# Norms by pairs of columns, first products interleaved, and low parts of weights by accumulating DMA, in a two-part transformer on one core

## The chip, the cores and the metric

The kernel runs on one core of a Trainium2 chip. The metric is the device time of one launch in microseconds, by the median of several runs; the profiled execution is one more run. TensorE does the matrix products (PE), VectorE (DVE), ScalarE (ACT) and GpSimd (POOL) the rest; SyncE (SP) issues most of the DMAs.

## The reference

A first block of two layers (differential attention with the modulation of both contexts, then neighbourhood attention, each followed by an MLP) hands x, 512 tokens of width 1024, to a second block of two layers. All of it is float32.

```python
def second_block(x, meta_tokens, w_in, w_ret_o, ...):
    h = jnp.concatenate([meta_tokens, x], axis=1)             # 16 + 512 tokens
    for l in range(DEPTH):
        u = rms_norm_2(h, norm_mix_pre[l])
        proj = u @ w_in[l]                                    # split into q, k, v, g of both branches, two gates
        ...
        y_r = retention_branch(...) @ w_ret_o[l]
        y_a = attention_branch(...) @ w_att_o[l]
        mix = (jax.nn.sigmoid(gate_r) * y_r + jax.nn.sigmoid(gate_a) * y_a) @ w_mix_o[l]
        h = h + rms_norm_2(mix, norm_mix_post[l])
        u = rms_norm_2(h, norm_ff_pre[l])
        ff = jnp.square(jax.nn.relu(u @ w_ff1[l])) @ w_ff2[l]
        h = h + rms_norm_2(ff, norm_ff_post[l])
    return h[:, N_META:]
```

## The kernel before

Activations lie transposed, 128 features by tokens, eight tiles k deep. Float32 products are made of three: every operand is a high part rounded to PE's format and a low part, the rest (`split` L214 for activations, by ACT and DVE), and `mm3` (L219, its matmul is L228) adds high x high, high x low and low x high. bigB and bigC are the high and low part of a normed input; bigA, the residual; bigD and bigF another such pair.

Weights come through `wring` (L235): SP loads a [128, 1024] tile `wr` (512 KB), ACT copies it into the high part `wh` (L207), and another engine, POOL unless the call names one, subtracts it to give the low part `wl` (L253):

```python
            self.act(h[:, c], r[:, c], AF.Copy)
            ...
                eng.tensor_tensor(l[:, q], r[:, q], h[:, q].bitcast(F32), op=ALU.subtract)
```

There are five buffers of `wh` and `wl` and two of `wr` (eight and three in the MLP stages).

The tokens are worked in two groups (`eg`: 272 or 256 tokens, and 256). A stage ends in a norm: `rstd` (L375) squares the eight k on ACT into `nt`, adds them on DVE into `na`, sums over partitions with a product by `ones` on PE (L384) into `n`, and makes 1/sqrt on ACT into `nr`. `norm_gain` (L399, L403) and `norm_mod` (L390) multiply and split into bigB and bigC, k by k. In `block2` the part behind the mix products (L1375 on) does this for the post-norm (L1393, the old residual `xo` loaded just before it) and the norm of the MLP; `after` (L1412) does it at the end of a layer, where half of the additions to bigA run on POOL (L1421) and `b2_norm` and `front` (L1086) begin the next layer with the first products of `k`, `q` and two gates.

`mlp` (L796) goes over eight chunks c of the hidden width, each with four first products (`first`), a squared relu into `hh` and `hl`, and eight second ones. In chunks 1 to 6 of three of the four MLPs `product7` (L853) takes seven products of sums of weights and inputs in place of eight. The sums of inputs (`sums`, L826) are made behind chunk 0, k by k, by POOL and DVE in turn; those of weights by POOL (L269).

The order on each engine is set by a scheduler from the program's text and its own estimates of durations; each engine then takes its instructions in that order. A tile's buffers are handed out in turn, so an instruction that writes a tile also waits for the readers of the tile that had the buffer before.

Stages, in us of the profiled execution: the first block to about 1520, its last output products and norm to 1640, MLP to 1885, front to 1945, then for the first layer of the second block retention to 2175, attention to 2335, mix to 2400, mix products, norms and chunk 0 to 2565, MLP to 2835, end norms and front to 2945; for the second layer retention to 3110, attention to 3268, mix to 3360, norms and chunk 0 to 3500, MLP to 3760, end.

Of the kernel before, what the change touches and what calls it, by code (L numbers as in the profile page):

```python
# [10 lines left out]
F32 = mybir.dt.float32  # L11
F32R = mybir.dt.float32r
BF16 = mybir.dt.bfloat16
AF = mybir.ActivationFunctionType
# [160 lines left out]
class Program:  # L175
# [59 lines left out]
    def wring(self, *parts, size=1024, low=None, eng=None):  # L235
# [10 lines left out]
        def parts(r, c, eng):  # L246
# [9 lines left out]
        def load(src, c=slice(0, size)):  # L256

            r = raw()
            self.nc.sync.dma_start(r[:, c], src)
            return parts(r, c, eng or self.G)  # L260
# [113 lines left out]

    def rstd(self, pl, X, n):  # L375

        pv = self.pt("n")[:, :n]
        acc = self.tl(pl, "na", [128, self.nw], 1)[:, :n]
        for k in range(8):
            sq = acc if k == 0 else self.tl(pl, "nt", [128, self.nw], self.nb)[:, :n]  # L380
            self.act(sq, X[:, k], AF.Square)
            if k:
                self.tt(acc, acc, sq, ALU.add)
        self.T.matmul(pv, self.ones, acc, start=True, stop=True)  # L384
        r = self.tl(pl, "nr", [128, self.nw], self.nb // 2)[:, :n]
# [4 lines left out]
    def norm_mod(self, pl, i, c, X, n, j, hh, hl):  # L390
        A, B = self.modA[i, c + 1], self.modT[i][:, c]
        r = self.rstd(pl, X, n)
        for k in range(8):
# [5 lines left out]
    def norm_gain(self, pl, X, n, g, hh, hl):  # L399
        r = self.rstd(pl, X, n)  # L400
        for k in range(8):
# [21 lines left out]
    def decays(self, pl):  # L423
# [10 lines left out]
        for c in (slice(0, 528), slice(528, 1055)):  # L434
            n = c.stop - c.start
            d = self.tl(pl, "delta", [16, 528], 1)[:, :n]
            nc.scalar.dma_start(d, self.ap["delta"][:, c].to_broadcast([16, n]))
            f = self.tl(pl, "fdec", [16, 528], 1)[:, :n]
# [6 lines left out]
    def layer0(self):  # L445
# [5 lines left out]
        with st:  # L451
            wp = st.enter_context(self.phase("l0w"))
            load = self.wring((wp, 5, 2), size=768)
# [26 lines left out]
            with self.psum(n=(1, 2), pj=(1, 6)), self.phase("l0n") as pn:  # L480
                self.nw, self.nb = 512, 4
# [241 lines left out]
    def post(self, i):  # L723
# [13 lines left out]
        with self.psum(a=(1, 6), n=(1, 2)), self.phase("pw") as wp, self.phase("post") as pl:  # L737
            load = self.wring((wp, 8, 2), eng=V) if both else self.wring((self.wp, 5, 2), (wp, 3, 1))
            self.nw, self.nb = (512, 3) if both else (336, 5)
# [56 lines left out]
    def mlp(self, pl, load, w1, w2, width, gs, fin, after, fast=None, before=None):  # L796
# [21 lines left out]

        def second(m, c, us, gs, hid):
# [6 lines left out]
        def sums():  # L826
# [782 lines left out]
```

## Time and profile before

| what | us |
|---|---|
| median of 3 runs | 3780.08 (3775.22 to 3780.64) |
| the profiled execution | 3780.57 |
| its span | 3778.6 |
| PE busy | 3476.2 (92%) |
| DVE busy | 2447.4 (65%) |
| POOL busy | 1938.6 (51%) |
| ACT busy | 1892.2 (50%) |

Busy shares are means over the whole span, in which stages with different limits follow each other. PE's 92% leaves about 300 us in which it does nothing; beside that, a product lasts longer when the granted clock (PEclk, 1.00 is full speed) is low. A wait names the engine, the line and what it waited for.

### The profile page before, as it was taken

The numbers are of one execution on the slowest core, as the hardware profiler recorded it, in microseconds if no ns is written. First come the engines' busy times: TensorE is split into PE (matmuls) and PEld (weight loads), VectorE is DVE, ScalarE is ACT, GpSimd is POOL, SyncE is SP. The second block draws the span as 40 slices with busy tenths as digits, with TensorE's granted clock in tenths as the row PEclk, the third lists the DMA queues.
The fourth block names the chain that finished last, engine by engine and source line by source line (L and its number), as shares of the span: only waits on it lengthen the run. The fifth ranks groups of instructions, "written<-read, shape, count | busy, mean of one in ns | idle before, by whom it ended". The sixth has DMA issues, their size and how long they took to land.

```text
span 3778.6 us, 58735 instructions
## 1 busy us (share of the span) xinstructions
PE 3476.2 (92%) x22512; PEld 3186.2 (84%) x22512; DVE 2447.4 (65%) x4189; ACT 1892.2 (50%) x3915; POOL 1938.6 (51%) x1754
## 2 busy tenths in 40 slices
PE   7888888899999999799989999979997999998998
PEld 6788876778888998788889899979997888787888
DVE  5666657433335777777677666496667767558766
ACT  5777755332125877533346665443334666543333
POOL 5778765442002665587732332457763233356884
PEclk9999999999999999999999999989998999999999
DMA  5222133442112222223322221323332222241333
GB/s 196 74 73 73 59 104 99 140 134 95 56 56 73 58 61 67 81 90 95 123 95 71 78 76 52 116 78 95 96 124 84 82 89 73 59 135 64 101 95 106
DMA packets 118571, 338.04 MB, mean 89 GB/s; under 512 B 13905, under 2 KB 37330, under 8 KB 118034
## 3 DMA queue, kind: packets, MB, share of 16 engines
q1 hardware_dynamic: 105664, 315.97, 26.7%
q10 hardware_dynamic: 12626, 18.32, 1.5%
q8 instruction: 176, 2.88, 0.3%
q14 instruction: 105, 0.86, 0.1%
HBM read 321.39 MB, written 12.86 MB: 88 GB/s over the span
## 4 chain that ended last, share of the span: by engine, by line
PE 49%; DVE 18%; POOL 13%; DMA 7%; ACT 6%; issue 6%; ACTq 0%; POOLq 0%; SPq 0%; DVEq 0%
PE a L228 38%; POOL wmu L345 9%; DMA wmg<-in_wmod 5%; PE pj L228 4%; DVE ms L888 3%; POOL wl L253 2%; DVE hl L217 2%; DVE ms L212 1%; DVE nt L212 1%; ACT wh L207 1%; DVE na L212 1%; PE po L1311 1%; ACT wmu L209 1%; DVE bigC L217 1%; DVE nt L403 1%
## 5 line engine op out<-in xcount | busy, mean ns | idle before, releaser
L253 POOL TENSOR_TENSOR wl<-wr,wh 128x256 fp32r<-128x256 f32 (+3 forms) x568 | 994.3, 1770 | 1031.8 <-ACT wh L207 902.7
L207 ACT ACTIVATE wh<-wr 128x1024 fp32r<-128x1024 f32 (+3 forms) x560 | 536.0, 972 | 731.8 <-PE a L228 387.4
L228 PE MATMUL a<-bigB,wh 128*128 128x256 f32 (+3 forms) x2140 | 637.3, 316 | 27.0 <-ACT bigB L216 17.2
L228 PE MATMUL a<-bigC,wh 128*128 128x256 f32 (+3 forms) x2140 | 645.6, 316 | 7.6 <-DVE bigC L217 7.6
L228 PE MATMUL a<-bigB,wl 128*128 128x256 f32 (+3 forms) x2140 | 642.1, 315 | 0.4 <-DVE wl L253 0.4
L345 POOL TENSOR_TENSOR wmu<-wmg,sc 128x256 f32<-128x256 f32 x512 | 420.3, 852 | 268.6 <-DMA wmg<-in_wmod 196.2
L228 PE MATMUL a<-hl,wh 128*128 128x256 f32 (+2 forms) x1664 | 492.8, 333 | 23.3 <-DVE hl L217 23.2
L228 PE MATMUL a<-hh,wh 128*128 128x256 f32 (+2 forms) x1664 | 466.2, 333 | 42.7 <-ACT hh L216 33.1
L228 PE MATMUL a<-hh,wl 128*128 128x256 f32 (+2 forms) x1664 | 487.0, 331 | 0.0
L228 PEld LDWEIGHTS a<-bigB,wh 128*128 128x128 f32 x2140 | 397.6, 193 | 54.4 <-ACT bigB L216 19.1
L228 PEld LDWEIGHTS a<-bigC,wh 128*128 128x128 f32 x2140 | 399.5, 192 | 33.8 <-DVE bigC L217 10.2
L228 PEld LDWEIGHTS a<-bigB,wl 128*128 128x128 f32 x2140 | 399.0, 193 | 24.7 <-DVE wl L253 1.1
L228 PEld LDWEIGHTS a<-hh,wh 128*128 128x128 f32 x1664 | 287.4, 192 | 81.1 <-ACT hh L216 38.2
L228 PEld LDWEIGHTS a<-hl,wh 128*128 128x128 f32 x1664 | 296.6, 193 | 63.6 <-DVE hl L217 35.4
L253 DVE TENSOR_TENSOR wl<-wr,wh 128x1024 fp32r<-128x1024 f32 (+1 forms) x144 | 201.0, 1405 | 184.8 <-ACT wh L207 184.3
L228 PEld LDWEIGHTS a<-hh,wl 128*128 128x128 f32 x1664 | 296.3, 193 | 27.2
L228 PE MATMUL a<-bigF,wh 128*128 128x256 f32 (+3 forms) x1024 | 295.0, 294 | 2.3 <-ACT bigF L216 2.3
L217 DVE TENSOR_TENSOR hl<-ms,hh 128x512 fp32r<-128x512 f32 (+4 forms) x160 | 190.2, 1207 | 80.0 <-ACT hh L216 79.4
L209 ACT ACTIVATE wmu<-wmu 128x1024 f32<-128x1024 f32 x128 | 135.3, 1057 | 201.7 <-POOL wmu L345 201.0
L228 PEld LDWEIGHTS a<-bigF,wh 128*128 128x128 f32 x1024 | 194.2, 192 | 5.3 <-ACT bigF L216 2.5
L228 PE MATMUL a<-bigD,wh 128*128 128x256 f32 (+2 forms) x640 | 187.2, 303 | 6.6 <-ACT bigD L216 4.1
L228 PE MATMUL pj<-wh,bigB 128*128 128x384 f32 x512 | 182.2, 360 | 9.8 <-ACT raw L207 5.6
(350 smaller groups left out, 8541.3 us busy)
## 6 DMA issues: line engine op xcount, KB each, us to landing
wr<-in_w SPq DMA_DIRECT2D x128, 512.0 KB, 3.6
wr<-in_wf SPq DMA_DIRECT2D x128, 512.0 KB, 3.6
wmg<-in_wmod SPq DMA_DIRECT2D x80, 512.0 KB, 3.6
wr<-in_wfm SPq DMA_DIRECT2D x76, 512.0 KB, 3.5
wr<-in_wqkv SPq DMA_DIRECT2D x64, 384.0 KB, 3.2
wm<-in_wmod SPq DMA_DIRECT2D x16, 512.0 KB, 6.2
wr<-in_wv SPq DMA_DIRECT2D x16, 512.0 KB, 3.5
wr<-in_wret SPq DMA_DIRECT2D x16, 512.0 KB, 3.5
```

Of the source, the lines that this page charges most:

```text
L207: self.S.activation(o, i, f, bias=bias, scale=scale)
L209: self.S.activation(o, i, f, bias=bias, scale=scale, accum_out=accum)
L212: self.V.tensor_tensor(o, a, b, op=op)
L217: self.V.tensor_tensor(lo, src, hi.bitcast(F32), op=ALU.subtract)
L228: self.T.matmul(o, w, x, start=(i == 0 and j == 0), stop=(i == n - 1 and j == 2))
L253: eng.tensor_tensor(l[:, q], r[:, q], h[:, q].bitcast(F32), op=ALU.subtract)
L345: self.G.tensor_tensor(u[:, q:q + 256], w[:, q:q + 256], self.sc[:, j, q:q + 256], op=ALU.mult)
L403: self.V.scalar_tensor_tensor(t, X[:, k], g[:, k:k + 1], r, op0=ALU.mult, op1=ALU.mult)
L888: V.scalar_tensor_tensor(r[:, s], r[:, s], 0.0, r[:, s], op0=ALU.max, op1=ALU.mult)
L1311: T.matmul(po[g], x[:n, t - 1], y[:, s], start=False, stop=(t == 4 and j == 2))
```

## The change

All code of the second block, and the first block's second `post`, is touched; the first block's other stages keep their form (the calls there get `eng=G` and `pairs = False`).

Weights: with `eng=None` the low part is made by ACT (l = -h) and a DMA from POOL's queue that reads the weight again and adds it. This holds for all loads of front, retention, attention and mix (62 a layer) and for the eight weights of chunk 0 in three MLPs. Weights of the mix products (`wmix`) have their low part made on DVE.

```diff
+            if eng is None:
+                self.act(l[:, c], h[:, c].bitcast(F32), AF.Copy, scale=-1.0)
+                self.G.dma_start(l[:, c], src, accum_op=ALU.add)
+                return h, l
...
-        load = self.wring((self.wp, 5, 2))
+        load = self.wring((self.wp, 5, 2), eng=None)
...
+            how = dict(eng=None) if c == 0 and fast else {}
+            u1 = [(load.sums if quick else load)(w1[c * 4 + j], **how) for j in range(4)]
+            u2 = [load(w2[c * 4 + j], **how) for j in range(4)]
...
+            us = [load(ap["wmix"][li, m], eng=V) for m in range(8)]
```

Norms: two k at a time, [128, 544] tiles; the gain moves to the instruction behind.

```diff
+    def scaled(self, pl, X, r, n):
+
+        for k in range(0, 8, 2):
+            u = self.pair(pl, "nt", n)
+            self.tt(u, X[:, k:k + 2], r[:, None].to_broadcast([128, 2, n]), ALU.mult)
+            yield from ((k + i, u[:, i]) for i in range(2))
...
+            acc = self.pair(pl, "na", n, 1)
+            for k in range(0, 8, 2):
+                sq = self.pair(pl, "nt", n) if k else acc
+                self.act(sq, X[:, k:k + 2], AF.Square)
+                if k:
+                    self.tt(acc, acc, sq, ALU.add)
+            for i in range(2):
+                self.T.matmul(pv, self.ones, acc[:, i], start=(i == 0), stop=(i == 1))
...
-        for k in range(8):
-            t = self.tl(pl, "nt", [128, self.nw], self.nb)[:, :n]
-            self.V.scalar_tensor_tensor(t, X[:, k], g[:, k:k + 1], r, op0=ALU.mult, op1=ALU.mult)
-            self.split(hh[:, k], hl[:, k], t)
+        for k, u in self.scaled(pl, X, r, n):
+            self.act(hh[:, k], u, AF.Copy, scale=g[:, k:k + 1])
+            self.V.scalar_tensor_tensor(hl[:, k], u, g[:, k:k + 1], hh[:, k].bitcast(F32),
+                                        op0=ALU.mult, op1=ALU.subtract)
```

The post-norm takes the old residual from prefetched tiles (`old`: `hh`, `hl`, `rr`, `gr`; 12 DMAs a layer from POOL's queue); the end norm adds in the same instruction.

```diff
+            for m in range(8):
+                t = self.tl(pl, ("hh", "hl")[m % 2], [128, 528], 4)[:, :n0]
+                G.dma_start(t, spill[:, m, eg[0]])
...
+                t = self.tl(self.b5, ("rr", "gr")[m // 4], [128, 528], 2)[:, :2 * n1].rearrange("p (k t) -> p k t", k=2)
+                G.dma_start(t, spill[:, m:m + 2, eg[1]])
...
-                    xo = self.tl(pl, "xo", [128, 272], 3)[:, :n]
-                    nc.sync.dma_start(xo, spill[:, m, s])
...
+                for m, u in self.scaled(pl, A[:, :, s], r, n):
+                    V.scalar_tensor_tensor(A[:, m, s], u, g[:, m:m + 1], old[i][m], op0=ALU.mult, op1=ALU.add)
...
-                    V.scalar_tensor_tensor(t, Df[:, m, s], g[:, m:m + 1], r, op0=ALU.mult, op1=ALU.mult)
-                    (V, G)[m % 2].tensor_tensor(A[:, m, s], A[:, m, s], t, op=ALU.add)
+                for m, u in self.scaled(pl, Df[:, :, s], r, n):
+                    V.scalar_tensor_tensor(A[:, m, s], u, g[:, m:m + 1], A[:, m, s], op0=ALU.mult, op1=ALU.add)
```

`sums` works on pairs of k, all on DVE (28 instructions), and `norm_mod` on pairs too. Products between stages: `first2` (chunk 0) and `mmu2` (front) run two units k by k.

```diff
+        def first2(us, j, g, hid):
+
+            x = g[3]
+            ps = [self.pt("a")[:, :x.stop - x.start] for _ in range(2)]
+            for k in range(8):
+                for i, p in enumerate(ps):
+                    wh, wl = block(us, j + i, k)
+                    for y, (w, z) in enumerate(((wh, g[1]), (wh, g[2]), (wl, g[1]))):
+                        T.matmul(p, w, z[:, k], start=(k + y == 0), stop=(k == 7 and y == 2))
...
-        for _, u in units:
-            u.start()
-            u.run(u.groups[:1])
+        for a, b in ((units[0][1], units[1][1]), (units[2][1], units[3][1])):
+
+            for u in (a, b):
+                u.start()
+            for u, p in zip((a, b), mmu2(a.w, b.w, (a.groups[0], b.groups[0]))):
+                self.act(u.raw[:, u.groups[0]], p, AF.Copy)
```

DVE's order behind the mix products of the first layer, group 0, before (the numbers are of buffers, `na` the sum of squares, `nr` 1/sqrt):

```order
L212 TENSOR_TENSOR na_25437<-na_25437,nt_25451 128x272
L212 TENSOR_TENSOR na_25437<-na_25437,nt_25454 128x272
L212 TENSOR_TENSOR na_25437<-na_25437,nt_25457 128x272
L1393 SCALAR_TENSOR_TENSOR nt_25466<-bigA_72,vecs,nr_25461 128x272
L1393 SCALAR_TENSOR_TENSOR nt_25471<-bigA_72,vecs,nr_25461 128x272
L1393 SCALAR_TENSOR_TENSOR nt_25476<-bigA_72,vecs,nr_25461 128x272
L1393 SCALAR_TENSOR_TENSOR nt_25481<-bigA_72,vecs,nr_25461 128x272
L1393 SCALAR_TENSOR_TENSOR nt_25486<-bigA_72,vecs,nr_25461 128x272
L212 TENSOR_TENSOR bigA_72<-nt_25466,xo_25464 128x272
L212 TENSOR_TENSOR bigA_72<-nt_25471,xo_25469 128x272
```

The same place with the change:

```order
L257 TENSOR_TENSOR wl_25183<-wr_25180,wh_25182 128x1024
L212 TENSOR_TENSOR na_25395<-na_25395,nt_25400 128x544
L212 TENSOR_TENSOR na_25395<-na_25395,nt_25403 128x544
L212 TENSOR_TENSOR nt_25411<-bigA_72,nr_25408 128x544
L212 TENSOR_TENSOR nt_25415<-bigA_72,nr_25408 128x544
L212 TENSOR_TENSOR nt_25419<-bigA_72,nr_25408 128x544
L212 TENSOR_TENSOR nt_25423<-bigA_72,nr_25408 128x544
L1470 SCALAR_TENSOR_TENSOR bigA_72<-nt_25411,vecs,hh_25114 128x272
L1470 SCALAR_TENSOR_TENSOR bigA_72<-nt_25411,vecs,hl_25116 128x272
L1470 SCALAR_TENSOR_TENSOR bigA_72<-nt_25415,vecs,hh_25118 128x272
```

Sixteen instructions of one k give way to four of two k and eight of one; a subtraction for a mix weight stands among them.

POOL's order in the MLP of the first block's second layer, from the last weights of `post` on, before:

```order
L253 TENSOR_TENSOR wl_15078<-wr_15075,wh_15077 128x256
L253 TENSOR_TENSOR wl_15449<-wr_15446,wh_15448 128x1024
L253 TENSOR_TENSOR wl_15455<-wr_15452,wh_15454 128x1024
L253 TENSOR_TENSOR wl_15461<-wr_15458,wh_15460 128x1024
L253 TENSOR_TENSOR wl_15467<-wr_15464,wh_15466 128x1024
L253 TENSOR_TENSOR wl_15473<-wr_15470,wh_15472 128x1024
```

With the change:

```order
L257 TENSOR_TENSOR wl_15078<-wr_15075,wh_15077 128x256
L252 DMA wl_15395<-in_w 128x1024
L252 DMA wl_15402<-in_w 128x1024
L252 DMA wl_15409<-in_w 128x1024
L252 DMA wl_15416<-in_w 128x1024
L252 DMA wl_15423<-in_w 128x1024
```

POOL issues a DMA for each weight of chunk 0 where it subtracted; its part of the sums of inputs, which followed, is gone.

And among the retention's output weights, the first prefetches of the old residual, on POOL with the change:

```order
L252 DMA wl_23711<-in_wfm 128x1024
L252 DMA wl_23772<-in_wret 128x1024
L1456 DMA rr_25130<-spill_0_18841 128x2x256
L252 DMA wl_23937<-in_wret 128x1024
L1456 DMA rr_25132<-spill_0_18841 128x2x256
L252 DMA wl_24098<-in_wret 128x1024
```

They stand between the low parts of weights that attention uses, on the same queue.

## Rows read from the trace of the kernel before

**Rows 1.** The page: busy us of each engine, the chain that ended last.

```profile
PE 3476.2 (92%) x22512; PEld 3186.2 (84%) x22512; DVE 2447.4 (65%) x4189; ACT 1892.2 (50%) x3915; POOL 1938.6 (51%) x1754
...
PE 49%; DVE 18%; POOL 13%; DMA 7%; ACT 6%; issue 6%; ACTq 0%; POOLq 0%; SPq 0%; DVEq 0%
```

**Rows 2.** Busy time by stretch, us from:to, length, then by the first row.

```profile
core 0: us, PE busy (x) PEld busy (x) DVE busy (x) ACT busy (x) POOL busy (x), PEclk, DMA share, GB/s
1520.00:1640.00 120.00, 98.20 (x718) 95.12 (x717) 96.58 (x156) 59.17 (x123) 77.95 (x58) 0.89 0.27 89
...
1945.00:2175.00 230.00, 214.06 (x1637) 205.39 (x1637) 160.85 (x339) 142.47 (x306) 67.51 (x33) 0.97 0.23 74
2175.00:2335.00 160.00, 152.85 (x1207) 148.77 (x1205) 109.98 (x342) 95.52 (x240) 45.71 (x20) 0.99 0.21 68
2335.00:2400.00 65.00, 65.00 (x508) 64.94 (x509) 24.32 (x29) 30.63 (x52) 26.37 (x13) 0.95 0.25 78
2400.00:2565.00 165.00, 141.98 (x1053) 137.05 (x1051) 128.60 (x192) 69.52 (x141) 86.59 (x60) 0.93 0.31 97
2565.00:2835.00 270.00, 262.25 (x2095) 257.12 (x2095) 174.38 (x238) 83.90 (x107) 190.60 (x128) 1.00 0.34 104
2835.00:2945.00 110.00, 86.45 (x621) 82.74 (x620) 86.14 (x155) 53.57 (x114) 39.41 (x32) 0.89 0.27 86
2945.00:3110.00 165.00, 162.03 (x893) 134.24 (x891) 119.83 (x203) 106.74 (x188) 52.98 (x27) 1.00 0.26 82
...
3360.00:3500.00 140.00, 117.94 (x819) 111.19 (x818) 113.32 (x185) 57.78 (x120) 85.25 (x63) 0.90 0.27 88
```

**Rows 3.** PE's waits from 1520, 2400, 2835, 3360 on: us, times, longest.

```profile
PE n L384 <- DVE na L212: 3.6, 1, 3.6
...
PE n L384 <- DVE na L212: 7.4, 1, 7.4
...
PE n L384 <- DVE na L212: 9.9, 1, 9.9
...
PE n L384 <- DVE na L212: 8.1, 2, 7.2
```

**Rows 4.** Timeline of DVE, 2435:2480: start us, us, instruction, idle before it.

```profile
2441.07 4.73 DVE L1393 SCALAR_TENSOR_TENSOR nt<-bigA,vecs,nr 128x272 f32<-128x272 f32 x5 [4.01 <-ACT nr L207]
...
2452.82 2.42 DVE L212 TENSOR_TENSOR bigA<-nt,xo 128x272 f32<-128x272 f32 x1 [0.56 <-DMA xo<-spill]
...
2464.38 2.15 DVE L403 SCALAR_TENSOR_TENSOR nt<-bigA,vecs,nr 128x272 f32<-128x272 f32 x5 [2.51 <-ACT nr L207]
...
2475.65 0.49 DVE L403 SCALAR_TENSOR_TENSOR nt<-bigA,vecs,nr 128x272 f32<-128x272 f32 x1
...
2477.44 0.43 DVE L217 TENSOR_TENSOR bigC<-nt,bigB 128x272 fp32r<-128x272 f32 x1
```

**Rows 5.** Timeline of POOL, 2435:2485, same columns.

```profile
2442.57 2.52 POOL L253 TENSOR_TENSOR wl<-wr,wh 128x1024 fp32r<-128x1024 f32 x1 [0.86 <-ACT wh L207]
...
2452.51 2.43 POOL L253 TENSOR_TENSOR wl<-wr,wh 128x1024 fp32r<-128x1024 f32 x1 [2.15 <-ACT wh L207]
```

**Rows 6.** DVE's forms in 2400:2565: busy us, mean ns, idle before.

```profile
L253 DVE TENSOR_TENSOR wl<-wr,wh 128x1024 fp32r<-128x1024 f32 x4 | 6.0, 1492 | 0.0
...
L217 DVE TENSOR_TENSOR bigF<-sg,bigD 128x528 fp32r<-128x528 f32 x2 | 1.4, 708 | 1.4 <-ACT bigD L216 1.4
```

**Rows 7.** POOL's forms from 1885 to the end, same columns.

```profile
L253 POOL TENSOR_TENSOR wl<-wr,wh 128x1024 fp32r<-128x1024 f32 x206 | 521.4, 2543 | 737.6 <-ACT wh L207 698.5 <-PE n L1539 18.4 <-PE a L228 15.0
```

**Rows 8.** Tile wh on ACT, 1945:2400: ns min/median/max, first and last start.

```profile
L207 ACT ACTIVATE wh<-wr x59: 631/1059/1063, 1947.6 to 2396.9; 128x1024 fp32r<-128x1024 f32 x51, 128x512 fp32r<-128x512 f32 x8
```

**Rows 9.** DMA queues and issues: KB each, median us to landing.

```profile
q1 hardware_dynamic: 105664, 315.97, 26.7%
...
wr<-in_w SPq DMA_DIRECT2D x128, 512.0 KB, 3.6
...
wm<-in_wmod SPq DMA_DIRECT2D x16, 512.0 KB, 6.2
```

More of the change, by code (lines that the diff above doesn't have):

```diff
@@ L254, in parts, with load @@
             return h, l
-        def load(src, c=slice(0, size)):
+        def load(src, c=slice(0, size), eng=eng):
             r = raw()
             self.nc.sync.dma_start(r[:, c], src)
-            return parts(r, c, eng or self.G)
+            return parts(r, c, eng, src)
         def sums(src):
@@ L392, in norm_mod @@
         r = self.rstd(pl, X, n)
+        if self.pairs:
+            for k in range(0, 8, 2):
+                u = self.pair(pl, "nt", n)
+                self.tt(u, X[:, k:k + 2], r[:, None].to_broadcast([128, 2, n]), ALU.mult)
+                for e in range(2):
+                    self.act(u[:, e], u[:, e], AF.Identity, bias=B[:, k + e, j:j + 1], scale=A[:, k + e, j:j + 1])
+                self.split(hh[:, k:k + 2], hl[:, k:k + 2], u)
+            return
         for k in range(8):
@@ L737, in post @@
         with self.psum(a=(1, 6), n=(1, 2)), self.phase("pw") as wp, self.phase("post") as pl:
[L738 to L739 removed]
+            load = self.wring((wp, 8, 2), eng=V) if both else self.wring((self.wp, 5, 2), (wp, 3, 1), eng=self.G)
+            self.nw, self.nb, self.pairs = (512, 3, False) if both else (272, None, True)
             if not both:
@@ L894, in mlp @@
                 before()
-            u1 = [(load.sums if quick else load)(w1[c * 4 + j]) for j in range(4)]
-            u2 = [load(w2[c * 4 + j]) for j in range(4)]
+            how = dict(eng=None) if c == 0 and fast else {}
+            u1 = [(load.sums if quick else load)(w1[c * 4 + j], **how) for j in range(4)]
+            u2 = [load(w2[c * 4 + j], **how) for j in range(4)]
             hid = [(self.tl(pl, "hh", [128, width], 4, F32R), self.tl(pl, "hl", [128, width], 4, F32R))
@@ L903, in mlp @@
             for i, part in enumerate(parts):
-                if not quick:
+                if c == 0:
+                    for j in (0, 2):
+                        first2(u1, j, part[0], hid)
+                elif not quick:
                     for j in range(4):
@@ L921, in layer1 @@
             pp, wp, kp, lp, pl = (st.enter_context(self.phase('l1' + n)) for n in 'pwkla')
-            load = self.wring((wp, 5, 2), size=768, low=lp)
+            load = self.wring((wp, 5, 2), size=768, low=lp, eng=G)
             half = (slice(0, 64), slice(64, 128))
@@ L1101, in mmu, with mmu2 @@
                            [B[:, k, s] for s in gs], [C[:, k, s] for s in gs]) for k in range(8)], hold)
+            return ps
+        def mmu2(w, x, gs):
+            ps = [self.pt("a")[:, :s.stop - s.start] for s in gs]
+            for k in range(8):
+                for p, (h, l), s in zip(ps, (w, x), gs):
+                    c = slice(k * 128, (k + 1) * 128)
+                    for j, (y, z) in enumerate(((h, B), (h, C), (l, B))):
+                        T.matmul(p, y[:, c], z[:, k, s], start=(k + j == 0), stop=(k == 7 and j == 2))
             return ps
```

95 lines of the change are left out of this document (52 added, 43 removed).

## The prediction

> **What bounds the kernel now.** I read the page first: TensorE (PE) is busy 92% of the span, and yet the chain that ended last is PE for only 49% of it and DVE and POOL for 31% [rows 1]. So there is waiting, and the question is where. The second view is the busy time by stretch [rows 2], one row for each stage from the end of the first block on. What a stage could give is PE's idle time plus what the lowered clock costs, (1 - PEclk) times the length. For the stretch that begins at 2400 this is 165 - 141.98 = 23.0, plus 0.07 x 165 = 11.6, together 34.6 us. The other three places where a norm stands between two products (1520, 2835, 3360) have 35.0, 35.7 and 36.1 by the same working, so the four have 141.4 us. The interior of an MLP (2565 to 2835) has 7.8, and the four stretches of retention, attention and mix shown have 22.8 + 8.8 + 3.3 + 3.0 = 37.9. The four transitions are what this kernel loses.
>
> The third view is what PE waited for in them [rows 3]: the longest single wait is each time the `ones` product at L384 for the sum of squares on DVE, 3.6 to 9.9 us. The fourth is DVE instruction by instruction behind 2435 [rows 4]. A SCALAR_TENSOR_TENSOR over 272 columns takes 0.49 us at 2475.65, but five of them from 2441.07 take 4.73, and one add at 2452.82 takes 2.42. Beside both of them stands POOL's subtraction of a weight, 2.52 and 2.43 us long [rows 5]. So DVE, which everybody waits for here, is itself held by POOL's instruction, about once for each weight.
>
> **The change part by part.** *Norms in pairs.* From the first L1393 of group 0 (2441.07) to the last write of bigC (2477.44 + 0.43) the chain takes 36.8 us [rows 4]. With the change the same piece is 4 + 3 + 4 TENSOR_TENSOR over 544 columns and 8 + 8 SCALAR_TENSOR_TENSOR over 272. The 544-column form is not in the trace; the 528-column one takes 0.708 us [rows 6], so by width 0.73, with 0.43 (no gain in a longer one) to 0.97 (two instructions of 0.49 end to end) as bounds. The sum is 11 x 0.73 + 16 x 0.49 = 15.9 us, and one wait for rsqrt between them, 2.51 us before [rows 4], and one matmul and a wider square more now, say 3.5. This makes 19.4 us, 47% less, provided nothing holds DVE. The bounds of the one price move it by 3 us either way. At the end of a block the eight additions, half of them on POOL now, go into the eight SCALAR_TENSOR_TENSOR, so DVE has 4 + 8 instructions there as before and waits for POOL no more.
>
> *First products interleaved.* Two units of chunk 0 take the k of the norm as it comes, so PE has twice as much to do for each k while the norm runs. It adds no instruction. What it is worth lies inside the same idle time, and I do not count it twice.
>
> *Sums of chunk 0 all on DVE.* 28 instructions over 512 or 528 columns at 0.708 [rows 6] = 19.8 us, where DVE had half of the pieces and POOL the other half. That is some 10 us more for DVE, three times. They stand behind group 1's norm, while PE runs chunk 0's second products and group 1's first ones; cost nothing while the norms save more than that on DVE in the same stretch (17 us for one group, above).
>
> *Lows of 24 weights of chunk 0 and 124 of front, retention, attention and mix by an accumulating DMA.* Removed: 148 POOL instructions of 2.54 us [rows 7]. Added: an ACT pass each, at the price of the first pass, 1.06 us by its median [rows 8], and one DMA from POOL's queue. The trace has no accumulating DMA. From below its price is that of a plain load of 512 KB, 3.6 us; from above twice the slowest load of that size, 2 x 6.2 = 12.4 us [rows 9]. I take twice the plain one, 7.2 us, since the weight is read and the tile is read and written, and the plain load of the same tensor is the nearest row. It is hidden as long as a weight is not needed sooner: in 1945 to 2400 there are 59 weights between 1947.6 and 2396.9 [rows 8], one each 7.75 us, and five pairs of buffers give four weights of lead, 31 us, against 3.6 + 1.06 + 1.06 + 7.2 = 12.9 us from the load to the finished low part. Queue traffic grows by 148 x 0.52 = 78 MB on 316 MB that take 26.7% of the engines [rows 9]: 7% more, no bound.
>
> The Trainium skill (SBUF — State Buffer, the trap "DVE blocks DMA" and § Who interferes with whom) speaks against this: a DMA from POOL's queue needs its descriptors written by GpSimd, and a DVE instruction in a two-port mode keeps it from writing them. It also says that tensor_tensor has no such mode. No run here shows either; by the first the sum would turn to rival C, by the second it stays.
>
> ACT's passes: 30 weights in the retention stage of layer 0 (230 / 7.75) are 32 us on 142.47 of 230; 124 in all are 131 us. DVE gets relief there, since POOL's subtractions are gone. I take both together at nothing for the stages from retention to mix: the cover is PE, busy 93 to 100% of them [rows 2], and if ACT is late the next wait is for `wh`.
>
> *Low parts of the 16 mix weights on DVE*, 1.49 us each [rows 6], 12 us a layer, and 24 prefetches of the old residual on POOL's queue in place of 32 just-in-time loads. The first lie in the mix stage, where DVE is busy 24.3 of 65 us and PE all of it [rows 2]. The prefetches for group 1 stand on POOL's queue between the accumulating DMAs of the retention's output weights and wait for the buffers `rr` and `gr`; a low part behind them waits too, with the 31 us of lead as cover. Both at nothing.
>
> *The sum.* The chain of a norm falls by 47%, and I give half of the four transitions' room: the wait at L384 and the idle time behind it shrink with the chain, and with shorter gaps the clock, 0.89 to 0.93 there against 1.00 in the MLP, falls less. 0.5 x 141.4 = 70.7 us, and 2 us for the interleaved front(0): 73. The profiled execution's 3780.6 less 73 is 3708; the median of the runs shown, 3780.1, is the same to half a microsecond, so the forecast is **3708 us**. Its own range: at the least the four waits at L384 alone, 7.4 + 9.9 + 7.2 (the longest of each) + 3.6 = 28 us, 3752; at the most three quarters of the room, 106 us, 3674.
>
> **The rivals.** *A, relief everywhere.* The DVE instructions of retention and attention are held in the same way, and half of their 38 us comes too; with two thirds of the transitions' room this is 19 + 94 = 113, 3667 us (3640 to 3684). For it: a `POOL` subtraction for each weight there as well. Against it: PE is busy nearly all of these stages, so little of DVE's delay reaches it.
>
> The Trainium skill (SBUF — State Buffer, § Who interferes with whom) has the rule behind A: a DVE instruction with two inputs in SBUF and a GpSimd instruction that reads SBUF exclude each other wholly. The trace agrees (2.42 us beside 2.43 [rows 4, 5]); where PE waits for something else it gives nothing.
>
> *B, ACT in the way.* Retention and attention have long chains over ACT, each of its passes stands in order, and a weight's second pass of 1.06 us goes in front of something PE waits for half of the time: 66 us of the 131 are given back, 3774 us (3752 to 3800), which is about no change. For it: ACT's 142 of 230 us in the first of these stages becomes 174. Against it: five buffers let the scheduler put the passes early.
>
> *C, the accumulating DMA is too slow.* If POOL's queue delivers one low part each p us, and one at a time, the stages from front to mix are bound by it from p = 7.75 on, and lose 124 x (p - 7.75). The gain of 73 is gone at p = 7.75 + 73/124 = 8.3 us. At 9 us the kernel is 155 - 73 = 82 us slower, 3863; at the upper bound, 12.4, it is 124 x 4.65 - 73 = 504 us slower. For it: the bound from above is 12.4, and 7.2 is an assumption; such a DMA must read what it adds to. Against it: the loads from SP of the same size overlap each other, and 16 engines are 27% busy.
>
> *D, nothing of it reaches PE*: DVE with all sums and no help from POOL is as late as before at group 1, and PE waits at the sums of chunk 0 in place of L384. Then only the four waits of 28 us are won, which is the lower end of the forecast and not another case.
>
> **How the numbers follow.** Forecast 0.57, A 0.13, B 0.15, C 0.15. Two executions of this kernel can be told apart from about 0.2%, 7.6 us, so faster means under 3772.5. The forecast and A are faster whole; B's range is half below that, a third within, the rest above: 0.07, 0.05, 0.03. Faster 0.77, same 0.05, slower 0.18. The range 3655 to 3795 holds the forecast, most of B and two thirds of A, and leaves out C and the low end of A, about 0.2. Cases of both signs are not evenly weighted, and the likeliest one's own range is 3674 to 3752.
>
> **What would show it.** In the four transitions of the new profile PE's idle time is near half of 21.8, 23.0, 23.6 and 22.1 us and the clock 0.95 or more; the wait of L384 is below 4 us; group 0's chain in ffw takes about 20 us and no DVE instruction lasts 2.4 us. In 1945 to 2400 PE is as busy as before, ACT about 60 us busier; `wl` does not appear among PE's waits. Wrong would be: waits of PE for a DMA into `wl`, which is C, or for ACT's passes, which is B, a longer retention stage by more than 10 us, or transitions with the same idle time behind the sums, which is D.

## The result, and the profile after

| | before | with the change |
|---|---|---|
| median of 4 runs, us | 3780.36 (3775.22 to 3780.92) | 3731.35 (3728.44 to 3732.34) |
| ratio | | 0.9872, 95% interval 0.9855 to 0.9889 |
| span of the profiled execution, us | 3778.6 | 3726.5 |

The kernel is 49 us faster where 73 were forecast, inside the range, but with the gain in other places than the prediction put it. The page of the changed kernel, in the parts of busy time, DMA queues, chain and DMA issues, answers [rows 1, 9]:

```profile
PE 3454.1 (93%) x22548; PEld 3166.7 (85%) x22548; DVE 2262.3 (61%) x4045; ACT 2004.4 (54%) x3959; POOL 1638.3 (44%) x1686
...
q1 hardware_dynamic: 101056, 311.71, 26.4%
q0 software_dynamic: 22720, 77.67, 12.0%
...
PE 57%; DVE 13%; POOL 11%; DMA 8%; ACT 6%; issue 4%; ACTq 0%; SPq 0%; POOLq 0%; DVEq 0%
...
wl<-in_wfm POOLq DMA_DIRECT2D x76, 512.0 KB, 6.2
```

POOL has lost 300 us and DVE 185, ACT has gained 112. A new queue, q0, carries the accumulating DMAs and the prefetches; an accumulating one of 512 KB lands after 6.2 us by the median of the 76 shown, where the forecast took 7.2. In the chain, DVE and POOL fell from 31% to 24% and PE rose from 49% to 57%.

The busy time by stretch, with the columns of [rows 2], cut where the same work begins and ends:

```profile
1517.00:1635.00 118.00, 96.75 (x738) 94.29 (x738) 84.50 (x128) 65.46 (x108) 46.77 (x39) 0.88 0.47 128
...
1932.00:2150.00 218.00, 208.94 (x1631) 200.92 (x1632) 134.38 (x340) 163.52 (x333) 25.32 (x33) 0.99 0.61 143
2150.00:2305.00 155.00, 152.51 (x1211) 148.96 (x1209) 95.33 (x342) 113.18 (x258) 18.69 (x22) 0.99 0.61 135
2305.00:2370.00 65.00, 64.74 (x511) 64.48 (x511) 18.63 (x34) 38.12 (x65) 11.01 (x13) 0.96 0.72 158
2370.00:2531.00 161.00, 139.09 (x1072) 135.92 (x1071) 108.23 (x160) 76.73 (x129) 61.42 (x48) 0.95 0.44 122
...
2799.00:2900.00 101.00, 84.76 (x611) 79.77 (x611) 61.17 (x130) 61.17 (x109) 13.90 (x24) 0.92 0.54 140
2900.00:3066.00 166.00, 162.89 (x899) 135.23 (x899) 102.50 (x202) 123.38 (x207) 20.24 (x28) 1.00 0.64 150
...
3312.00:3448.00 136.00, 114.89 (x828) 108.87 (x828) 101.08 (x151) 63.80 (x107) 64.34 (x46) 0.94 0.41 111
```

PE's idle time plus the loss by the clock, worked out as in the prediction, is 35.4, 30.0, 24.3 and 29.3 us in the four transitions (1517, 2370, 2799, 3312), where it was 35.0, 34.6, 35.7 and 36.1. So 22 of their 141 us are won and not 71, and none in the first. What PE waits for there, for the stretches 1517:1635, 2370:2531, 2799:2900 and 3312:3448 in turn (total, times, longest), answers [rows 3]:

```profile
PE a L860 <- ACT bigB L216: 11.4, 1, 11.4
...
PE a L860 <- ACT bigB L207: 10.1, 1, 10.1
PE a L228 <- DVE hl L217: 7.0, 3, 6.2
...
PE n L401 <- DVE na L212: 6.2, 1, 6.2
...
PE a L1311 <- DMA wl<-in_wv: 1.9, 1, 1.9
PE a L1166 <- DMA wl<-in_wfm: 1.9, 1, 1.9
...
PE a L860 <- ACT bigB L207: 9.7, 1, 9.7
```

The wait for the `ones` product is gone in three of the four, and in these another of 10 to 11 us stands in its place: the first products (L860) wait for the first bigB, which ACT writes. Group 0's norm behind the mix products of the first layer shows why it does there. DVE's timeline, beside [rows 4]:

```profile
2410.91 2.63 DVE L212 TENSOR_TENSOR nt<-bigA,nr 128x544 f32<-128x544 f32 x4 [4.55 <-ACT nr L207]
2413.46 0.50 DVE L1470 SCALAR_TENSOR_TENSOR bigA<-nt,vecs,hh 128x272 f32<-128x272 f32 x1
...
2426.47 2.63 DVE L212 TENSOR_TENSOR nt<-bigA,nr 128x544 f32<-128x544 f32 x4 [6.22 <-ACT nr L207]
2439.09 0.92 DVE L436 SCALAR_TENSOR_TENSOR bigC<-nt,vecs,bigB 128x272 fp32r<-128x272 f32 x2 [9.98 <-ACT bigB L207]
2440.86 5.28 DVE L436 SCALAR_TENSOR_TENSOR bigC<-nt,vecs,bigB 128x272 fp32r<-128x272 f32 x6 [0.85 <-ACT bigB L207]
```

The instructions have about the price that the prediction gave them: four of 544 columns in 2.63 us, 0.50 for one of 272. Only the last row is slower, six in 5.28 us, since one of them lasts 2.7 us beside POOL, which sums weights of the next chunk from 2441.3 on. But the chain from 2410.9 to the end of the last bigC at 2446.1 takes 35.2 us where 19.4 were forecast and 36.8 were before. DVE works in 17.1 us of it and waits for ACT in 18.2, of which 10.0 lie in one piece before the first bigC. ACT's timeline, same place:

```profile
2426.03 0.41 ACT L207 ACTIVATE nr<-nr 128x272 f32<-128x272 f32 x1
2437.32 1.06 ACT L207 ACTIVATE wh<-wr 128x1024 fp32r<-128x1024 f32 x1 [10.88 <-DMA wr<-in_wf]
...
2438.55 0.92 ACT L207 ACTIVATE bigB<-nt,vecs 128x272 fp32r<-128x272 f32 x2
```

ACT takes its instructions in order, and ahead of bigB stands the copy of a weight that had not landed: 10.88 us for `wr<-in_wf`. The load was late while the DMA engines were full. The DMA view of 2405:2445 (first line: busy tenths in 40 slices of 1 us), and the landing of the loads into `wr` in 2415:2445:

```profile
DMA  0000699599997999999999999999999983000989
...
q0 software_dynamic: 973, 3.59, 50.1%
q1 hardware_dynamic: 1904, 4.26, 30.6%
...
wl<-in_wf POOLq DMA_DIRECT2D x7, 512.0 KB, 9.0
...
DMA to landing us min/median/max: 5.7/11.8/17.1
```

From 2413 to 2437 every slice but one is at 90% or more. The accumulating DMAs of chunk 0 take half of the 16 engines' time for 3.59 MB, the plain transfers 31% for 4.26 MB. The accumulating ones land in 9.0 us, and the loads in up to 17.1, where the median load of `in_wf` takes 3.6 over the whole execution. Behind the mix products of the second layer it is the same: ACT waits 10.7 us for `wr<-in_wf` in front of its first bigB.

In the first transition the reason is another. ACT waits for loads 1.2 us in all there (1535:1570). Its order has all eight passes of the modulated norm (`norm_mod`), and copies of chunk 0's weights among them, ahead of the first bigB, which starts 15.2 us behind the `ones` product; before it was 5.9 us. The wait for bigB is 7.1 to 11.7 us there in all runs with the new norms, whoever makes the low parts, and 2.6 and 2.9 in the two with the old ones; that it comes from the order is read from the trace, and no run changes the order alone.

To see where the rest went, the execution is cut at events that every kernel has: the first `ones` product of a norm (for "retention", the first and the last but one `ones` product of the retention's own norms), read from PE's timeline. Lengths in us of the profiled executions; the runs are told below.

| stage | before | changed | no accum. DMA | before + accum. | chunk 0 on DVE | all on DVE | mixed |
|---|---|---|---|---|---|---|---|
| norm of the first block, its MLP | 360.1 | 356.6 | 361.5 | 361.4 | 357.2 | 359.1 | 358.0 |
| end norm, front(0) | 87.7 | 75.9 | 93.3 | 74.3 | 75.1 | 84.8 | 80.6 |
| retention, layer 0 | 178.2 | 172.8 | 174.1 | 172.8 | 172.8 | 165.7 | 163.7 |
| attention and mix, layer 0 | 267.6 | 261.2 | 266.9 | 262.0 | 261.2 | 263.4 | 264.0 |
| post-norm, norm, MLP, layer 0 | 406.4 | 401.0 | 399.5 | 406.5 | 396.7 | 396.5 | 396.7 |
| end norm, front(1) | 107.7 | 97.0 | 104.0 | 96.9 | 95.0 | 96.5 | 97.7 |
| retention, layer 1 | 154.7 | 158.2 | 154.9 | 157.6 | 158.3 | 158.4 | 154.0 |
| attention and mix, layer 1 | 256.3 | 250.8 | 255.8 | 252.3 | 251.9 | 254.2 | 251.7 |
| post-norm, norm, MLP, layer 1 | 382.0 | 378.3 | 374.5 | 383.2 | 370.3 | 370.3 | 370.4 |

The stages in front of the first row, which the change leaves alone, took 1542 to 1549 us in these executions, so a difference below 3 us in a row is not read; the end, some 32 us, is left out.

### The profile page after: what moved, and what is told of

The parts are those of the page before. It is cut to its first block, busy times and chain, and to the rows that moved or that the text cites. A ratio compares the mean times of both kernels' runs of the same rounds, so it can differ in the third digit from the quotient of the medians.

```text
span 3726.5 us, 58703 instructions
## 1 busy us (share of the span) xinstructions
PE 3454.1 (93%) x22548; PEld 3166.7 (85%) x22548; DVE 2262.3 (61%) x4045; ACT 2004.4 (54%) x3959; POOL 1638.3 (44%) x1686
## 3 DMA queue, kind: packets, MB, share of 16 engines
q1 hardware_dynamic: 101056, 311.71, 26.4%
q0 software_dynamic: 22720, 77.67, 12.0%
## 4 chain that ended last, share of the span: by engine, by line
PE 57%; DVE 13%; POOL 11%; DMA 8%; ACT 6%; issue 4%; ACTq 0%; SPq 0%; POOLq 0%; DVEq 0%
PE a L228 41%; POOL wmu L349 8%; PE pj L228 7%; DMA wmg<-in_wmod 5%; DVE ms L939 3%; DVE nt L212 2%; POOL wl L257 2%; DVE hl L217 2%; DVE ms L212 1%; PE a L860 1%; ACT wh L207 1%; DMA wr<-in_wf 1%; PE po L1379 1%; PE po L1112 1%; ACT wmu L209 1%
## 5 line engine op out<-in xcount | busy, mean ns | idle before, releaser
L257 POOL TENSOR_TENSOR wl<-wr,wh 128x256 fp32r<-128x256 f32 (+2 forms) x404 | 601.2, 1513 | 356.2 <-ACT wh L207 281.5
L228 PE MATMUL a<-bigB,wh 128*128 128x256 f32 (+3 forms) x1852 | 557.9, 317 | 10.2 <-ACT wh L207 7.8
L228 PE MATMUL a<-bigC,wh 128*128 128x256 f32 (+3 forms) x1852 | 555.6, 315 | 0.7 <-DVE bigC L436 0.7
L228 PE MATMUL a<-bigB,wl 128*128 128x256 f32 (+3 forms) x1852 | 554.8, 315 | 0.4 <-DVE wl L257 0.4
L228 PE MATMUL a<-hh,wh 128*128 128x256 f32 (+2 forms) x1664 | 462.2, 332 | 30.8 <-ACT hh L216 18.2
L228 PEld LDWEIGHTS a<-bigB,wh 128*128 128x128 f32 x1852 | 340.9, 191 | 36.3 <-ACT wh L207 8.5
L228 PEld LDWEIGHTS a<-bigC,wh 128*128 128x128 f32 x1852 | 340.8, 190 | 22.9 <-DVE bigC L436 0.9
L228 PEld LDWEIGHTS a<-bigB,wl 128*128 128x128 f32 x1852 | 340.5, 190 | 22.9 <-DVE wl L257 1.1
L228 PEld LDWEIGHTS a<-hl,wh 128*128 128x128 f32 x1664 | 295.5, 192 | 71.1 <-DVE hl L217 42.8
L257 DVE TENSOR_TENSOR wl<-wr,wh 128x1024 fp32r<-128x1024 f32 (+1 forms) x160 | 220.4, 1387 | 214.4 <-ACT wh L207 207.6
L228 PEld LDWEIGHTS a<-hh,wh 128*128 128x128 f32 x1664 | 284.2, 191 | 68.4 <-ACT hh L216 22.1
L252 POOL DMA_DIRECT2D wl<-in_wfm x76 | 65.4, 860 | 534.5 <-ACT wl L207 351.8
L216 ACT ACTIVATE hh<-ms 128x512 fp32r<-128x512 f32 (+4 forms) x160 | 89.9, 587 | 200.6 <-DVE ms L939 129.1
```

Of the source, the lines that this page charges most:

```text
L216: self.S.activation(hi, src, AF.Copy)
L228: self.T.matmul(o, w, x, start=(i == 0 and j == 0), stop=(i == n - 1 and j == 2))
L252: self.G.dma_start(l[:, c], src, accum_op=ALU.add)
```

## The experiments

All times are medians; ratios are to the kernel before, measured beside each run.

**Chunk 0 by POOL again.** Theory S, that the full DMA engines cost 10 us in each transition, against R, that ACT and DVE set the norm's length.

```diff
-            how = dict(eng=None) if c == 0 and fast else {}
+            how = {}
```

> The changed kernel, with the 24 low parts of chunk 0 made by POOL's subtraction again (no second ACT pass, no accumulating DMA there); all else as changed. Theory S (in the three transitions with chunk 0 the DMA engines are full, 99% busy for 27 us, because accumulating DMAs and plain loads of eight weights come at once; ACT waits in its order for a late load, and PE 10 to 11 us for bigB): those three waits of 11.4, 10.2 and 9.7 us fall below 4 each, and the time to 3706 to 3714 us. Rival R (the chain of the norm is as long as ACT and DVE make it, and POOL's subtractions hold DVE again as before): 3731 to 3745 us, with DVE instructions of 2.4 us in the transitions.

3732.1 us, ratio 0.9872 (0.9851 to 0.9894), four runs from 3724.9 to 3741.6: no difference to the changed kernel. In 2400:2500 PE's wait of 10 us for bigB is gone as S has it, but others are back, as R has it (PE's waits: total, times, longest):

```profile
PE a L860 <- DVE bigC L436: 4.4, 2, 3.6
PE n L401 <- DVE na L212: 3.1, 1, 3.1
```

Both were half right: the accumulating DMAs cost here about what POOL's subtractions cost. In this run the chain of group 0 takes 33.0 us.

**Front to mix by POOL again**, chunk 0 as changed.

```diff
-        load = self.wring((self.wp, 5, 2), eng=None)
+        load = self.wring((self.wp, 5, 2), eng=self.G)
```

> The changed kernel, with the 124 low parts of front, retention, attention and mix made by POOL's subtraction again; chunk 0 keeps the accumulating DMAs. Theory M (the accumulating DMAs free DVE in these stages and that reaches PE: the traces show 23 us less from the first front to the mix products of both layers): 3750 to 3758 us. Rival N (the gain in these stages comes from the norms before them and the interleaved first products, DVE's relief is used up by ACT's second passes): 3728 to 3736 us.

3765.9 us, ratio 0.9964 (0.9952 to 0.9975): 35 us slower than the changed kernel, more than M's 23 and outside of its range. The 124 accumulating DMAs that the forecast took at nothing carry most of the gain. Two places in the DVE timeline of this run, behind the end norm of the first block, and POOL beside them:

```profile
1905.07 6.83 DVE L212 TENSOR_TENSOR nt<-bigA,nr 128x544 f32<-128x544 f32 x4 [2.66 <-ACT nr L207]
...
1914.14 5.91 DVE L436 SCALAR_TENSOR_TENSOR bigC<-nt,vecs,bigB 128x272 fp32r<-128x272 f32 x4
```

```profile
1904.80 5.25 POOL L257 TENSOR_TENSOR wl<-wr,wh 128x1024 fp32r<-128x1024 f32 x2 [20.96 <-ACT wh L207]
1914.85 4.91 POOL L257 TENSOR_TENSOR wl<-wr,wh 128x1024 fp32r<-128x1024 f32 x2 [4.80 <-ACT wh L207]
```

The same instructions in the changed kernel:

```profile
1901.81 2.63 DVE L212 TENSOR_TENSOR nt<-bigA,nr 128x544 f32<-128x544 f32 x4 [2.66 <-ACT nr L207]
...
1907.33 1.73 DVE L436 SCALAR_TENSOR_TENSOR bigC<-nt,vecs,bigB 128x272 fp32r<-128x272 f32 x4
```

Four products of 544 columns take 6.83 us beside two subtractions of POOL and 2.63 without them. The busy time by stretch from this norm to the first retention, with POOL's subtraction and then in the changed kernel:

```profile
1902.00:1994.00 92.00, 80.38 (x621) 78.54 (x621) 67.80 (x108) 47.62 (x94) 34.08 (x26) 0.93 0.31 102
```

```profile
1899.00:1975.00 76.00, 73.42 (x576) 71.41 (x575) 42.81 (x101) 54.56 (x102) 14.90 (x24) 0.98 0.79 192
```

DVE's busy time falls from 67.8 to 42.8 us with nearly the same instructions, and the stage from 92 to 76. A rival would be that POOL is too slow and its low parts come too late. The trace speaks against it: with POOL's subtraction PE and its weight loads wait for no low part of POOL from 1880 to 3378, and ACT waits for POOL to free one in three places, 6.5 us in all.

**No accumulating DMA at all**: both edits together. It leaves the norms, the interleaved products, the sums, the prefetches and the mix weights' low parts on DVE.

> The changed kernel without any accumulating DMA: all 148 low parts by POOL again. It leaves the norms in pairs, the interleaved first products, the sums on DVE and the prefetched residual. Theories S and M together: 3731 - 22 + 23, that is 3728 to 3738 us. S with N: 3706 to 3714. R with M: 3755 to 3770 us.

3765.6 us, ratio 0.9961 (0.9947 to 0.9976). This is R with M: all parts but the DMAs give 14.5 us (9 to 20 by the interval), not 73. By the table they shorten the last MLP row of each layer by 7 us and lengthen front(0) by 6. Group 0's chain on DVE behind the mix products, and POOL beside its second half:

```profile
2443.78 4.85 DVE L212 TENSOR_TENSOR nt<-bigA,nr 128x544 f32<-128x544 f32 x4 [4.55 <-ACT nr L207]
2448.55 2.63 DVE L1470 SCALAR_TENSOR_TENSOR bigA<-nt,vecs,hh 128x272 f32<-128x272 f32 x1
...
2462.91 7.31 DVE L212 TENSOR_TENSOR nt<-bigA,nr 128x544 f32<-128x544 f32 x4 [4.58 <-ACT nr L207]
2470.15 6.94 DVE L436 SCALAR_TENSOR_TENSOR bigC<-nt,vecs,bigB 128x272 fp32r<-128x272 f32 x8
...
2462.64 5.20 POOL L257 TENSOR_TENSOR wl<-wr,wh 128x1024 fp32r<-128x1024 f32 x2 [2.08 <-ACT wh L207]
```

From 2443.8 to 2477.1 this is 33.3 us: POOL holds DVE as before, so that four products take 7.31 us and not 2.63, and one of 0.5 takes 2.63. The condition that the prediction put beside its 19.4 us, "provided nothing holds DVE", does not hold without the other half of the change.

**Chunk 0's low parts on DVE.**

```diff
-            how = dict(eng=None) if c == 0 and fast else {}
+            how = dict(eng=V) if c == 0 and fast else {}
```

> The changed kernel, with the 24 low parts of chunk 0 subtracted on DVE (1.4 us each, 11 us a transition), no second ACT pass and no accumulating DMA there. Theory S: the loads come in time as with POOL's subtraction, nothing holds DVE but its own 11 us, of which a part is hidden: 3704 to 3722 us. Rival R (DVE's work is the bound of the norm): 3735 to 3760 us, each transition 3 to 10 us longer than in the changed kernel.

3718.3 us, ratio 0.9843 (0.9822 to 0.9865): S, and by its median faster than the changed kernel. Group 0's chain, with seven weights' subtractions inside it, and PE's waits of 2400:2500:

```profile
2411.42 2.63 DVE L212 TENSOR_TENSOR nt<-bigA,nr 128x544 f32<-128x544 f32 x4 [1.35 <-ACT nr L207]
...
2426.77 2.49 DVE L257 TENSOR_TENSOR wl<-wr,wh 128x1024 fp32r<-128x1024 f32 x2 [2.84 <-ACT wh L207]
2429.82 2.63 DVE L212 TENSOR_TENSOR nt<-bigA,nr 128x544 f32<-128x544 f32 x4 [0.56 <-ACT nr L207]
...
2434.05 4.80 DVE L436 SCALAR_TENSOR_TENSOR bigC<-nt,vecs,bigB 128x272 fp32r<-128x272 f32 x8
```

```profile
PE a L228 <- DVE hl L217: 7.0, 2, 6.3
PE a L860 <- DVE bigC L436: 2.8, 1, 2.8
PE a L860 <- ACT bigB L207: 2.0, 1, 2.0
```

The chain takes 27.4 us (2411.4 to 2438.9), bigB is waited for 2.0 us and not 10.1. The wait for the low part of the hidden values is as long as in the changed kernel, 6.3 us. The transition behind the mix products of the second layer goes the same way, with 1.7 us for bigB where it was 9.7. In the first transition (1517:1635) the wait stays, without an accumulating DMA and without a second ACT pass in chunk 0:

```profile
PE a L860 <- ACT bigB L216: 9.8, 1, 9.8
```

**The kernel before with the accumulating DMAs from front to mix alone.** The branch `eng is None` of the change's diff is put into `wring`, and front's ring uses it; nothing else is changed.

> The kernel before with one thing added: the 124 low parts of front, retention, attention and mix by ACT's negation and an accumulating DMA; norms, first products, sums and chunk 0 as before. Taken away from the changed kernel this part cost 34 us. If the two parts add up (theory): 3780 - 34 = 3746, within 3738 to 3754 us. If the accumulating DMAs only pay once the norms are short (rival): 3765 to 3782 us. If they alone carry the gain and the norms only repair something: under 3738.

3749.2 us, ratio 0.9916 (0.9901 to 0.9931): 30 us from these DMAs alone, against 35 when they are taken from the changed kernel. The parts nearly add up: 30 and 14.5 are 45 of the 49 us.

**First products one unit after the other**, as before.

```diff
-                if c == 0:
-                    for j in (0, 2):
-                        first2(u1, j, part[0], hid)
-                elif not quick:
+                if not quick:
...
-            for u, p in zip((a, b), mmu2(a.w, b.w, (a.groups[0], b.groups[0]))):
-                self.act(u.raw[:, u.groups[0]], p, AF.Copy)
+        for _, u in units:
+            u.start()
+            u.run(u.groups[:1])
```

> The changed kernel with the first products one unit after the other, as before, in chunk 0 and in front. If the interleaving hides a norm's pace of k (theory): each of the five places gets 2 to 5 us longer, 3741 to 3756 us. Rival: PE waits for the first bigB anyway, in one piece of 10 us, and the order behind it is worth nothing: 3727 to 3736 us.

3731.3 us, ratio 0.9872 (0.9858 to 0.9887): the interleaving is worth nothing here, the rival. In 2400:2500 of this run PE waits 11.3 us in one piece for the first bigB and 0.8 for a bigC behind it, against 10.1 and 0.8 in the changed kernel: there are no gaps of note between the k that a second unit could fill.

**Accumulating DMAs for the first six weights of a layer alone**, POOL for the other 56.

```diff
-        load = self.wring((self.wp, 5, 2), eng=None)
+        ring, order = self.wring((self.wp, 5, 2), eng=None), count()
+
+        def load(src, c=slice(0, 1024)):
+            return ring(src, c, eng=None if next(order) < 6 else self.G)
```

> The changed kernel, but of the 62 weights a layer from front to mix only the first six (front's four and the next two) have an accumulating DMA, the other 56 POOL's subtraction. Theory F (the 34 us lie where POOL's subtractions of front's weights hold DVE beside the norm: the landmarks of the run with all on POOL put 23 of 37 us there): 3739 to 3750 us. Rival (relief everywhere, in proportion to the weights: 6 of 62): 3760 to 3768 us.

3754.1 us, ratio 0.9927 (0.9910 to 0.9943). A tenth of the weights brings 12 of the 35 us, and by the same cuts the two front stages are 79.0 and 99.0 us long, nearly the changed kernel's; but retention got 4 us longer in each layer than with POOL throughout (177.3 and 159.0 against 172.9 and 154.7), so the time lands between theory and rival. The front stages are the main place, not the only one.

**Half of the sums back on POOL**, on top of chunk 0 on DVE.

```diff
+                e = (V, G)[k // 2]
...
-                    self.tt(o, x[0], y[0], ALU.subtract)
+                    e.tensor_tensor(o, x[0], y[0], op=ALU.subtract)
```

> The run with chunk 0's low parts on DVE, and with the second half of the sums of inputs on POOL again, in pairs of k. In that run PE waits 6.3, 5.7 and 4.0 us for a low part of hidden values that stands behind the sums on DVE. If DVE's 20 us of sums are what it waits for (theory): each of these falls by half or more, 3705 to 3714 us. Rival: POOL's pieces hold DVE as its subtractions did, and the wait stays: 3716 to 3728 us.

3725.5 us, ratio 0.9853 (0.9838 to 0.9868): no better than 3718.3, the rival. The wait for the low part of hidden values falls from 4.0 to 2.8 us in the first transition and stays at 6.2 and 6.0 in the two behind the mix products. Giving POOL a half of these sums did not free DVE.

**Chunk 0 with ACT's second pass, but the weight added on DVE** (chunk 0's loads get `eng=0`).

```diff
+            if eng == 0:
+                self.act(l[:, c], h[:, c].bitcast(F32), AF.Copy, scale=-1.0)
+                self.tt(l[:, c], l[:, c].bitcast(F32), r[:, c], ALU.add)
+                return h, l
```

> The changed kernel, with the 24 low parts of chunk 0 made by ACT's negation as there, but the weight added on DVE from the loaded tile in place of the accumulating DMA. It keeps the second ACT pass and takes the DMA away. Theory S (the full DMA engines are what chunk 0's transitions wait for): as with DVE's subtraction, 3714 to 3724 us, and no wait of PE for bigB over 5 us behind the mix products. Rival (the second ACT passes in front of the norm's own are it): 3728 to 3740 us with the waits of 10 us still there.

3725.5 us, ratio 0.9852 (0.9835 to 0.9869). It lies just above S's 3714 to 3724, and PE's wait for bigB in 2400:2500 halves:

```profile
PE a L864 <- ACT bigB L207: 4.6, 1, 4.6
```

10.1 us in the changed kernel, 4.6 with the ACT pass and no DMA, 2.0 with neither. In this transition the DMA is about two thirds of what falls away and ACT's pass the rest, and in 3312:3448 the three waits are much the same, 9.7, 4.1 and 1.7. In the first transition they are 11.4, 9.6 and 9.8, so there the DMA is a small part at most. Of the time of all three the run leaves the share open: 3725 lies between 3718 and 3731, and the intervals overlap.

**All low parts on DVE**, none on POOL, no accumulating DMA.

```diff
-        load = self.wring((self.wp, 5, 2), eng=None)
+        load = self.wring((self.wp, 5, 2), eng=V)
```

and chunk 0 on DVE as above.

> The changed kernel with no accumulating DMA and nothing for POOL to subtract: all 148 low parts on DVE at 1.4 us each, 31 of them (44 us) in the first retention stage, where DVE was busy 134 of 218 us. Theory P (what the accumulating DMAs were worth is that POOL no longer holds DVE): the front stages keep their gain and the others lose some of it to DVE's own 174 us: 3715 to 3740 us. Rival (POOL was simply too busy or late, and DVE is as bad a place): 3750 to 3785 us.

3725.9 us, ratio 0.9858 (0.9837 to 0.9879): theory P. Without a single accumulating DMA the kernel is as fast as with 148 of them. Chunk 0 on DVE is in this, which gave 3718.3 and 3722.5 beside accumulating DMAs in front to mix, so there DVE is the worse place by 3 to 8 us. With PE's waits above, which have none for POOL's low parts, this says that what they were worth is, in the main, that POOL does not read beside DVE. The first retention, with all low parts on DVE and then in the changed kernel:

```profile
1986.00:2151.00 165.00, 159.28 (x1227) 152.72 (x1226) 123.32 (x282) 109.83 (x241) 2.94 (x7) 0.99 0.24 73
```

```profile
1975.00:2148.00 173.00, 166.06 (x1299) 159.18 (x1299) 110.00 (x278) 130.69 (x272) 20.16 (x27) 1.00 0.58 136
```

DVE takes 13 us more there and ACT 21 less, and the stage is 7 us shorter by the table. In front(0) the accumulating DMA stays better (75.9 against 84.8 us).

**Chunk 0 on DVE once more**, for the interval.

> The kernel with chunk 0's low parts on DVE once more, for a tighter interval, since it was the fastest: 3714 to 3724 us, against 3731 of the changed kernel. If the first measurement was favoured by chance: 3724 to 3734 us.

3722.5 us, ratio 0.9837 (0.9814 to 0.9860): the gain over the changed kernel is 9 to 13 us by the two medians, though the interval of each still touches the changed kernel's.

**Mixed**: the first six weights from front on by accumulating DMA, all others and chunk 0 on DVE.

```diff
-        load = self.wring((self.wp, 5, 2), eng=None)
+        ring, order = self.wring((self.wp, 5, 2), eng=None), count()
+
+        def load(src, c=slice(0, 1024)):
+            return ring(src, c, eng=None if next(order) < 6 else self.V)
```

> The changed kernel with an accumulating DMA for the first six weights from front on alone, and all other low parts, chunk 0's too, on DVE. From the stages of the earlier runs: front as with the accumulating DMAs (76 us, where DVE alone gave 85), the first retention as with DVE (166, where they gave 173), chunk 0 as with DVE: 3705 to 3717 us, the fastest of all. If these parts don't add up, because each changes the order on ACT and DVE of the next: 3718 to 3732 us.

3715.8 us (3714.7 to 3720.9), ratio 0.9830 (0.9816 to 0.9843): the fastest by its median, 64 us below the kernel before and 15.6 below the changed one, with its interval apart from the changed kernel's. The parts add up but for front(0), 80.6 us where 75.9 had been expected.

## Why the prediction was right, and where it was not

*The bound.* That DVE is held by POOL's subtractions of weights beside the norms was right, and it is most of the result: take POOL's reads away from front to mix by accumulating DMAs and 30 to 35 us are won [rows 4, 5], of 49 in all. The run with front to mix by POOL shows it the other way round, and with all 148 low parts on DVE 40 us are won against all on POOL (3725.9 and 3765.6). One reading behind it was wrong: in the first transition the wait at L384, 3.6 us, was not the longest; PE waited 4.1 for bigD and 3.9 for hh there.

*The norms in pairs: half of the transitions' room, 71 us.* This step failed. The prices were right (0.66 and 0.50 us measured for 0.73 and 0.49), the chain was not: 35.2 us against 19.4. DVE's own work in it was near the sum, 17.1 us for 15.9; the term that failed is the waiting, taken at 3.5 us and measured at 18.2, all of it for ACT. Chunk 0's weights, 24 of the 148, were still to be dealt with by someone at that very place: by ACT with a late load in the changed kernel, by POOL holding DVE without accumulating DMAs (33.3 us), or by DVE itself (27.4). In the first transition, by the trace, ACT's order of the modulated norm does the same. So PE's idle time in the four transitions is 21.3, 21.9, 16.2 and 21.1 us where half of 21.8, 23.0, 23.6 and 22.1 was to show, and the clock reached 0.95 in one of them. Beside POOL's subtractions the norms with sums, prefetches and mix weights are worth 14.5 us.

*The accumulating DMAs of front to mix: nothing.* This step failed too, the other way: 30 to 35 us. The prediction asked whether PE was busy in those stages [rows 2] and found 93 to 100%. But its table of room had no row for front(0), to which it gave 2 us and which brought 12 to 17 by the cuts, and front(1) was counted among the norms. Rival A, relief everywhere, has a part of it: 5 to 6 us in attention and mix of each layer.

*Chunk 0's accumulating DMAs: 7% more traffic, no bound.* The mean over the span was the wrong figure, and low: q0 took 12.0% of the engines' time for its 77.67 MB. In the 25 us in which chunk 0's weights come, the DMA engines are full, and ACT's order passes the delay on to the norm. Against POOL's subtraction it is even, against DVE's it costs 9 to 13 us.

*The price of one.* 7.2 us assumed, 5.7 to 7.6 measured in front to mix (medians of the tensors with 512 KB a weight) and 9.0 in the burst. PE waits for such a DMA 1.9 us twice; rival C did not come about. The Trainium skill's trap (SBUF — State Buffer, "The 'DVE blocks DMA' trap (SWDGE)") by which a DVE instruction in a two-port mode would keep GpSimd from writing the descriptors of POOL's queue, is not seen here. POOL's issue took 0.85 to 0.91 us for 124 of front to mix; whether such an instruction stood beside one of them no run shows. Rival B is not shown either: ACT has 16 us more in the first retention stage (130.7 in 1975:2148, 114.6 in the same work before), which got 5 us shorter; the second got 3.5 us longer, and with all low parts on DVE it did so too, so ACT's passes are not shown to be the cause.

*The interleaving* was counted at nothing beside the norms, but for 2 us in front(0), and measured at nothing (front(0) takes 75.3 us without it, 75.9 with it).

*Rival D*, that the sums on DVE take the place of L384, was there in part: PE waits about 6 us for a low part behind them in each of the three transitions. Before, it waited 5.4 for such a low part in one of them, and moving half of the sums to POOL did not help behind the mix products.

So the forecast came near by two errors against each other: 71 us for 14.5, and 0 for 30 to 35.

## What to carry to other kernels

Count who works beside the critical engine, not only how long its own instructions are; a row with one instruction at five times its price points to an engine beside it. Price a resource in the stretch where the work comes in a burst, not by its mean over the span. And where a change has two halves, cost each half with the other one missing: a condition such as "nothing holds it" belongs to one of them.

## What was not expected of the hardware

An accumulating DMA takes 1.8 times the DMA engines' time of a plain one for the same bytes: 77.67 MB in 12.0% of the span against 311.71 MB in 26.4%, that is 0.154% against 0.085% for a MB. The plain prefetches, some 4 MB, are in the first figure; in the kernel before with the accumulating DMAs alone on that queue it is 60.83 MB in 9.6%, 0.158%, which gives 1.9 times. Beside POOL's subtraction an instruction of DVE with two inputs lasts as long as the subtraction, also when it has 544 columns (four in 6.83 us beside two of POOL in 5.25), so joining two k to one instruction shortened the chain by only 3.5 us as long as POOL subtracted back to back (36.8 us before, 33.3 with pairs).
